# A third w_out tile in the broadcast pool, and residual loads tied to the first square sum, in the FFN down projection of a two-layer decoder trunk

## The chip, the cores and the metric

The kernel runs on one core of a Trainium2 chip. The time is the device time of one execution in microseconds (us); before and after are compared by the median of their runs. Engines are named as in the profile: PE (TensorE), PEld (its weight loads), DVE (VectorE), ACT (ScalarE), POOL (GpSimd) and SP, whose queue issues the DMAs of this kernel. L665 is line 665 of the kernel before. In the changed kernel the same lines have numbers 2 to 7 higher: the residual load is L381 before and L383 after, the matmul of the down projection L665 and L671, the load of H L622 and L624, that of w_out L626 and L632.

## What is computed

Two decoder layers over x of 1024 positions by 1024 channels, all in float32. Layer 0 mixes tokens with a chunked gated MLP, layer 1 with RWKV-7; each goes on with a cross attention into 256 memory rows and a SwiGLU feed-forward block (FFN), and each sub-layer is wrapped in two norms. Cut to what the change touches:

```
def rms_norm(x, g):
    xf = x.astype(jnp.float32)
    y = xf * lax.rsqrt(jnp.mean(xf * xf, axis=-1, keepdims=True) + RMS_EPS)
    return (y * g.astype(jnp.float32)).astype(x.dtype)

def swiglu_ffn(x, w_in, w_out):
    gate, up = jnp.split(x @ w_in, 2, axis=-1)
    return (jax.nn.silu(gate) * up) @ w_out

# every sub-layer:  x <- x + post_norm(f(pre_norm(x)))
```

The hidden width D_FF is 2816, so `w_out` is 2816 by 1024. The down projection is the last product, and the closing of a tile is the post norm, the addition to x (the residual) and the pre norm of the next sub-layer.

## The kernel before

**Numbers.** A float32 matmul is made of three: each operand is split into a rounded high part and a low part (`split`: a cast on ACT, L118, then a subtraction on DVE, L119), and high by high, high by low and low by high are summed in PSUM. In the down projection the high part is called `wh` and the low part `wl`, for H and for the weights alike; each step's two operands are split as a *unit* of two casts and two subtractions.

**The FFN.** `ffn` computes the gate and the up projection column block by column block and writes the hidden values, already combined, to seven DRAM buffers `hd` (`scr<-a` in the profile, L506 to L522). `ffn_out` then forms the down projection as seven products instead of eight (Strassen's scheme over 2 by 2 blocks): products 1, 2, 5, 6, 3, 7, 4 in this order, each in NS = 6 steps over D_FF (step 0 has one block of 128 rows per half, steps 1 to 5 two). A step has 12 or 24 matmuls of 128x128 by 512, so a product has 132. `load(q)` fetches one step's H tile into pool `wr` (3 buffers) and, in products 1, 2, 5 and 6, its rows of w_out. The loads run AHEAD = 3 steps before the matmuls. For product 1 the rows of steps 0 and 1 go into pool `s7` (2 buffers, called `s` in the profile); all other w_out tiles go into the large pool `a` of 32 buffers, which the gate stage also uses. `combine` later forms the other products' weights out of these tiles in place, on DVE. Pool `gb` has two buffers that hold gains broadcast over the partitions; in an FFN one of them holds the gains of its own post norm (`gpost`), the other the gains of the cross attention before it, whose last reader is that sub-layer's end (DVE, L430).

**Closing.** When a product completes a 128 by 512 block of the output, `evac` copies or adds it into tile y, and `finish` squares it on ACT (L677, the sum goes to a column of the group's small tile) and multiplies it by `gpost` on DVE (L678). The output tiles form groups: in layer 0 four groups of two tiles (nn = 2), in layer 1 eight groups of one. When all blocks of a group are there, a task made by `close` is queued: it takes a buffer `xr` per tile from the pool `t4` (4 buffers, called `t` in the profile), loads the residual rows into it from DRAM on SP (L381), forms the norm factor, adds on DVE (L390) and stores on SP (L391). In layer 0 it goes on with the next pre norm (L401, L403) and transposes.

**What sets the order.** The kernel is written as a sequence, with queued tasks run between its pieces (`tick`), but a scheduler decides where an instruction stands on its engine, by what it depends on and by its own estimate of time. An engine, SP included, then takes its instructions in that order. The residual load depends on nothing that the group computes; it needs only a free `t4` buffer, so the scheduler is free to put it far ahead of the rest of `close`. In layer 1 product 4 is split ahead into resident `a` tiles (`resident`), of which most are made while product 7 runs.

## Time and profile before

| | |
|---|---|
| median of 3 runs | 3202.71 us (3199.85 to 3232.83) |
| profiled execution | 3209.07 us, of which the span is 3207.2 us |
| mean granted PE clock in it | 0.967 |
| PE busy | 3080.7 us, 96% of the span |
| DVE, ACT, POOL busy | 1816.4, 1483.7 and 794.9 us |
| down projection, layer 0 | about 1067 us (first L665) to 1310 us |
| down projection, layer 1 | about 2967 us to the end |

Rows of a timeline give the start in us, the time in us, the engine, the line, the operation, what is written from what is read, and how often; in brackets the idle time before the row, and the instruction that ended it. SPq is the queue of SP, a DMA's row there being its issue and not its transfer. The chain that ended last is followed back from the end of the program, and its rows name the piece of work that was then the latest.

### The profile page before, as it was taken

To read this page: it belongs to the slowest core of one execution; us is meant where nothing else is said; L and a number is where in the kernel's file an instruction comes from. 1 tells how busy PE (TensorE), PEld (TensorE's weight loads), DVE (VectorE), ACT (ScalarE), POOL (GpSimd) and SP (SyncE) were. 2 spreads that over 40 slices of the span, in tenths; PEclk is the share of its full clock that TensorE was granted. 3 is DMA by queue.
4 is the path that set the end of the run, shared out by engine and by line. 5 is a ranking of instruction groups with operands and counts; after the bars stand their busy time and mean duration, and the time that the engine had idled before them with its cause. 6 is when DMAs were issued, how large, how long until landed. Compare 5 with 4: busy or idle time off the path is not lost.

```text
span 3207.2 us, 43874 instructions
## 1 busy us (share of the span) xinstructions
PE 3080.7 (96%) x16570; PEld 2519.9 (79%) x16570; DVE 1816.4 (57%) x2594; ACT 1483.7 (46%) x2751; POOL 794.9 (25%) x632
## 2 busy tenths in 40 slices
PE   8999999999999999999989899999999999999998
PEld 6788888778888777878767778887788778888776
DVE  5463544565555476655765667464545755554655
ACT  5433544633333345766753455355545533333443
POOL 0100011345555100111421121123011365554001
PEclk9999999999999999999998889699999999999999
DMA  5622535423333744744857633534553333333633
GB/s 191 204 74 71 192 118 167 158 75 100 105 99 98 251 137 132 226 127 146 266 184 197 191 105 87 150 97 164 180 165 134 110 109 99 99 99 125 233 113 130
DMA packets 434579, 457.59 MB, mean 143 GB/s; under 512 B 77696, under 2 KB 309280, under 8 KB 434368
## 3 DMA queue, kind: packets, MB, share of 16 engines
q1 hardware_dynamic: 427456, 429.62, 42.3%
q0 software_dynamic: 6912, 25.17, 2.5%
q8 instruction: 131, 2.15, 0.3%
q14 instruction: 80, 0.66, 0.1%
HBM read 332.48 MB, written 122.22 MB: 142 GB/s over the span
## 4 chain that ended last, share of the span: by engine, by line
PE 83%; DVE 6%; DMA 5%; issue 2%; ACT 2%; POOL 2%; SPq 1%; DVEq 0%; POOLq 0%; ACTq 0%
PE ps L459 26%; PE ps L148 11%; PE ps L150 11%; PE ps L149 11%; PE ps L665 11%; PE ck L1459 4%; PE ps L1356 2%; DVE wl L119 1%; PE ck L1472 1%; DMA a<-scr 1%; PE ps L1380 1%; DVE a L119 1%; PE ps L274 1%; DMA ld<-scr 1%; ACT wh L118 1%
## 5 line engine op out<-in xcount | busy, mean ns | idle before, releaser
L459 PE MATMUL ps<-a,wh 128*128 128x512 f32 x2464 | 772.3, 398 | 6.6 <-DVE a L119 5.4
L119 DVE TENSOR_TENSOR wl<-wr,wh 128x1024 fp32r<-128x1024 f32 (+1 forms) x417 | 481.5, 1165 | 460.4 <-ACT wh L118 454.9
L118 ACT CAST wh<-wr 128x1024 fp32r<-128x1024 f32 (+1 forms) x417 | 371.0, 901 | 601.1 <-PE ps L665 168.8
L459 PEld LDWEIGHTS ps<-a,wh 128*128 128x128 f32 x2464 | 465.6, 189 | 122.4 <-DVE a L119 7.0
L459 PE MATMUL ps<-a,wl 128*128 128x512 f32 x1232 | 480.7, 398 | 0.9 <-DVE wl L119 0.9
L148 PE MATMUL ps<-a,wh 128*128 128x512 f32 (+1 forms) x848 | 328.5, 392 | 9.7 <-ACT a L118 7.5
L148 PE MATMUL ps<-wh,a 128*128 128x512 f32 x800 | 316.0, 403 | 12.3 <-DVE a L430 4.1
L149 PE MATMUL ps<-a,wh 128*128 128x512 f32 (+1 forms) x848 | 324.9, 384 | 2.4 <-DVE a L119 2.4
L150 PE MATMUL ps<-a,wl 128*128 128x512 f32 (+1 forms) x848 | 324.5, 384 | 2.3 <-DVE wl L119 2.2
L149 PE MATMUL ps<-wl,a 128*128 128x512 f32 x800 | 318.6, 399 | 0.5 <-DVE wl L119 0.5
L150 PE MATMUL ps<-wh,a 128*128 128x512 f32 x800 | 316.1, 399 | 0.2 <-DVE a L119 0.2
L220 POOL TENSOR_TENSOR sm<-sm,mhalf 128x2 f32<-128x2 f32 (+3 forms) x68 | 72.2, 1065 | 922.3 <-DVE sm L240 847.6
L459 PEld LDWEIGHTS ps<-a,wl 128*128 128x128 f32 x1232 | 233.2, 189 | 58.1 <-DVE wl L119 1.4
L119 DVE TENSOR_TENSOR wl<-s,wh 128x512 fp32r<-128x512 f32 (+1 forms) x188 | 202.6, 1091 | 75.0 <-ACT wh L118 71.4
L665 PE MATMUL ps<-wl,wh 128*128 128x512 f32 x588 | 233.6, 397 | 10.3 <-DVE wl L119 10.3
L665 PE MATMUL ps<-wh,wl 128*128 128x512 f32 x588 | 231.9, 394 | 0.0
L118 ACT CAST wh<-s 128x512 fp32r<-128x512 f32 (+1 forms) x188 | 115.8, 633 | 205.2 <-PE ps L459 74.3
L665 PE MATMUL ps<-wh 128*128 128x512 f32 x588 | 198.2, 398 | 11.0 <-ACT wh L118 11.0
L148 PEld LDWEIGHTS ps<-a,wh 128*128 128x128 f32 x848 | 162.0, 192 | 43.5 <-ACT a L118 8.4
L150 PEld LDWEIGHTS ps<-a,wl 128*128 128x128 f32 x848 | 162.1, 191 | 37.0 <-DVE wl L119 4.0
L148 PEld LDWEIGHTS ps<-wh,a 128*128 128x128 f32 x800 | 151.8, 190 | 49.1 <-DVE a L430 5.0
L149 PEld LDWEIGHTS ps<-a,wh 128*128 128x128 f32 x848 | 162.7, 192 | 33.0 <-DVE a L119 2.7
(283 smaller groups left out, 5279.7 us busy)
## 6 DMA issues: line engine op xcount, KB each, us to landing
scr<-a SPq DMA_DIRECT2D x218, 256.0 KB
wr<-in_ffn_w_in SPq DMA_DIRECT2D x92, 512.0 KB
wr<-scr SPq DMA_DIRECT2D x70, 512.0 KB
scr<-t SPq DMA_DIRECT2D x58, 512.0 KB
wr<-in_rw_w_rkv SPq DMA_DIRECT2D x48, 512.0 KB
a<-in_ffn_w_out SPq DMA_DIRECT2D x38, 512.0 KB
ld<-scr SPq DMA_DIRECT2D x72, 256.0 KB
t<-scr SPq DMA_DIRECT2D x34, 512.0 KB
```

Of the source, the lines that this page charges most:

```text
L118: self.nc.scalar.copy(hi, src)
L119: (engine or self.nc.vector).tensor_sub(lo, src, hi)
L148: nc.tensor.matmul(out, lhsT=ah, rhs=bh, start=start, stop=False)
L149: nc.tensor.matmul(out, lhsT=ah, rhs=bl, start=False, stop=False)
L150: nc.tensor.matmul(out, lhsT=al, rhs=bh, start=False, stop=stop)
L220: self.nc.gpsimd.tensor_tensor(out=r, in0=v, in1=self.mhalf[:, 0:n], op=ALU.pow)
L274: nc.tensor.transpose(ps[:, t * P:(t + 1) * P], xs[t][:, k * P:(k + 1) * P], self.ident)
L459: self.nc.tensor.matmul(out, lhsT=a, rhs=b, start=start and k == 0 and (i == 0), stop=k == 3 and i == 2, skip_group_check=True)
L665: nc.tensor.matmul(ps, lhsT=a, rhs=b, start=i in (1, 2, 5) and n == 0 and k == 0 and z == 0, stop=n == NS - 1 and k == steps[n][1] - 1 and ...
L1356: nc.tensor.matmul(ps[:, c * P:(c + 1) * P], lhsT=BK[hs, q * 4 + c, :, :], rhs=AR[hs, q * 4 + c, :, :], start=True, stop=True)
L1380: nc.tensor.matmul(ps[0:64, o:o + 64], lhsT=GA[:, h, q * 4 + c, :], rhs=UV[:, q * 4 + c, h, :], start=True, stop=True)
L1459: mm = lambda o, l, r: nc.tensor.matmul(o, lhsT=l, rhs=r, start=False, stop=True, skip_group_check=True)
```

## The change

Two edits, both in `ffn_out` and in `close`.

1. For product 1 the w_out rows of step 2 go into the second buffer of pool `gb` instead of a buffer of pool `a`. The scheduler can place this load as soon as the cross attention's gains have been read for the last time.
2. `close` gets an argument `begun`: the column that the group's first square sum is written to. Before the residual load of a tile is issued, one element per partition of that column is copied into the first column of its `t4` buffer (DVE, 128x1). The load overwrites the copy, so it has to come after it, and thereby after the first square sum of the group. Other sub-layers call `close` without `begun` and are unchanged in this.

```
-        def close(tiles, hs, s):
+        def close(tiles, hs, s, begun=None):
...
             for t in tiles:
                 xr.append(self.tmp())
+                if begun is not None:
+                    nc.vector.tensor_copy(xr[-1][:, 0:1], begun)
                 nc.sync.dma_start(xr[-1], xin[t * P:(t + 1) * P, :])
...
-                W[b, a, n] = self.s7.tile([P, D], F32, name='s7', tag='s7') if b == a == 0 and n < 2 else self.a32()
+                if b == a == 0 and n < 3:
+                    pool, name = ((self.s7, 's7'), (self.s7, 's7'), (self.gb, 'gb'))[n]
+                    W[b, a, n] = pool.tile([P, D], F32, name=name, tag=name)
+                else:
+                    W[b, a, n] = self.a32()
                 nc.sync.dma_start(view(W[b, a, n], K), wv[b][:, c:c + K, a * 512:a * 512 + 512])
...
-        sums, done = ({}, {})
+        sums, done, begun = ({}, {}, {})
...
                 sums[group] = self.sums(nn)
                 done[group] = 0
+                begun[group] = sums[group][1][:, c:c + 1, tiles.index(t)]
...
-                self.later(close(tiles, [y[x] for x in tiles], s))
+                self.later(close(tiles, [y[x] for x in tiles], s, begun[group]))
```

The scheduler lays the instructions out anew. Four places follow, each before and then after.

SP at the start of layer 0's gate stage (`scr_93` is what the cross attention's closings store, `in_ffn_w_in` the gate stage's weights; layer 1 has the same):

```order
L381 DMA t_5050<-scr_92 128x1024
L471 DMA wr<-in_ffn_w_in 128x8x128 x2
L391 DMA scr_93<-t_4950 128x1024
L391 DMA scr_93<-t_4952 128x1024
L471 DMA wr<-in_ffn_w_in 128x8x128 x2
L391 DMA scr_93<-t_5048 128x1024
L391 DMA scr_93<-t_5050 128x1024
L471 DMA wr<-in_ffn_w_in 128x8x128 x5
```

```order
L383 DMA t_5050<-scr_92 128x1024
L473 DMA wr<-in_ffn_w_in 128x8x128 x2
L393 DMA scr_93<-t_4950 128x1024
L393 DMA scr_93<-t_4952 128x1024
L473 DMA wr<-in_ffn_w_in 128x8x128 x2
L632 DMA gb<-in_ffn_w_out 128x2x512
L393 DMA scr_93<-t_5048 128x1024
L393 DMA scr_93<-t_5050 128x1024
L473 DMA wr<-in_ffn_w_in 128x8x128 x5
```

The load into `gb` is new there, ahead of the last two stores of the cross attention and of the third batch of gate weights.

SP at the start of layer 0's down projection (`wr<-scr_5014` are the H tiles of product 1, `a<-in_ffn_w_out` the w_out tiles; layer 1 has the same):

```order
L626 DMA s_8193<-in_ffn_w_out 128x2x512
L622 DMA wr<-scr_5014 128x2x512 x2
L381 DMA t_9263<-scr_93 128x1024
L506 DMA scr_5014<-a 128x512
L622 DMA wr<-scr_5014 128x2x512
L381 DMA t_9265<-scr_93 128x1024
L381 DMA t_9355<-scr_93 128x1024
L622 DMA wr<-scr_5014 128x2x512 x2
L511 DMA scr_5015<-a 128x512
L512 DMA scr_5017<-a 128x512
L626 DMA a<-in_ffn_w_out 128x2x512
L516 DMA scr_5018<-a 128x512
```

```order
L632 DMA s_8193<-in_ffn_w_out 128x2x512
L624 DMA wr<-scr_5014 128x2x512 x2
L508 DMA scr_5014<-a 128x512
L624 DMA wr<-scr_5014 128x2x512 x3
L513 DMA scr_5015<-a 128x512
L514 DMA scr_5017<-a 128x512
L632 DMA a<-in_ffn_w_out 128x2x512
L518 DMA scr_5018<-a 128x512
```

The residual loads (L381) are gone from here; they now stand among the loads of H for product 5. The first load into an `a` buffer, in the same place behind the stores of `hd`, is that of step 2 before and that of step 3 after.

SP at the end of layer 1 (`out` is the kernel's output, `scr_20997` and `scr_20994`, or 21005 and 21002 after, the H tiles of products 7 and 4):

```order
L391 DMA out<-t_25233 128x1024
L622 DMA wr<-scr_20997 128x2x512
L381 DMA t_25595<-scr_96 128x1024
L391 DMA out<-t_25283 128x1024
L622 DMA wr<-scr_20997 128x2x512
L381 DMA t_25639<-scr_96 128x1024
L391 DMA out<-t_25318 128x1024
L391 DMA out<-t_25362 128x1024
L381 DMA t_25683<-scr_96 128x1024
L381 DMA t_25727<-scr_96 128x1024
L622 DMA wr<-scr_20994 128x512
L622 DMA wr<-scr_20994 128x2x512 x5
```

```order
L393 DMA out<-t_25241 128x1024
L624 DMA wr<-scr_21005 128x2x512
L393 DMA out<-t_25292 128x1024
L624 DMA wr<-scr_21005 128x2x512
L393 DMA out<-t_25328 128x1024
L393 DMA out<-t_25373 128x1024
L624 DMA wr<-scr_21002 128x512
L624 DMA wr<-scr_21002 128x2x512 x5
L383 DMA t_25607<-scr_96 128x1024
L383 DMA t_25652<-scr_96 128x1024
L383 DMA t_25697<-scr_96 128x1024
L383 DMA t_25742<-scr_96 128x1024
```

The four residual loads move from between the stores and the loads of H to behind the last load of H.

DVE in product 7 of layer 0 (`wl<-wr` and `wl<-a` are the two subtractions of a unit; L889, after it L896, scales two tiles of the memory rows for layer 1, which PE then transposes; L390, after it L392, is the closing's addition):

```order
L240 SCALAR_TENSOR_TENSOR sm<-sm 128x2
L403 TENSOR_SCALAR a<-t_9265,sm 128x1024
L119 TENSOR_TENSOR wl<-wr,wh 128x1024
L119 TENSOR_TENSOR wl<-a,wh 128x1024
L240 SCALAR_TENSOR_TENSOR sm<-sm 128x2 x2
L889 SCALAR_TENSOR_TENSOR a<-a,sm 128x1024 x2
L119 TENSOR_TENSOR wl<-wr,wh 128x1024
L390 SCALAR_TENSOR_TENSOR t_9355<-a,sm,t_9355 128x1024
L390 SCALAR_TENSOR_TENSOR t_9357<-a,sm,t_9357 128x1024
L119 TENSOR_TENSOR wl<-a,wh 128x1024
```

```order
L240 SCALAR_TENSOR_TENSOR sm<-sm 128x2
L405 TENSOR_SCALAR a<-t_9266,sm 128x1024
L240 SCALAR_TENSOR_TENSOR sm<-sm 128x2 x2
L896 SCALAR_TENSOR_TENSOR a<-a,sm 128x1024 x2
L119 TENSOR_TENSOR wl<-wr,wh 128x1024
L392 SCALAR_TENSOR_TENSOR t_9357<-a,sm,t_9357 128x1024
L392 SCALAR_TENSOR_TENSOR t_9360<-a,sm,t_9360 128x1024
L119 TENSOR_TENSOR wl<-a,wh 128x1024
```

One unit's two subtractions, which stood right behind L403, now stand behind the scalings and around the two additions. On PE the 16 transposes of the scaled tiles stand one step of product 7 earlier, behind the first four matmuls of the step that uses this unit.

## The prediction

> **What bounds the kernel now.** I read the page's head and its chain first, then who TensorE (PE) waits for, then the places where it waits, engine by engine. The span and the chain's shares by engine:

> ```profile
> span 3207.2 us, 43874 instructions
> ...
> PE 83%; DVE 6%; DMA 5%; issue 2%; ACT 2%; POOL 2%; SPq 1%; DVEq 0%; POOLq 0%; ACTq 0%
> ```

> PE carries 83% of the chain; an edit pays only where PE stands still or runs at a lower clock. The first row of PE's waits, by what ended them (total us, times, longest):

> ```profile
> PE ps L665 <- ACT wh L118: 11.0, 3, 3.9
> ```

> L665 is the matmul of the down projection. Three of its waits end with a cast on ACT and make 11.0 us. Where they lie, in the timeline of PE (start, us, idle before in brackets), followed by windows around them and around one shorter wait (busy us of PE, PEld, DVE, ACT, POOL; granted clock; DMA share; GB/s):

> ```profile
> 1081.87 2.08 PE L665 MATMUL ps<-wh 128*128 128x512 f32 x4 [3.63 <-ACT wh L118]
> ...
> 2981.70 2.08 PE L665 MATMUL ps<-wh 128*128 128x512 f32 x4 [3.87 <-ACT wh L118]
> ...
> 3155.90 2.08 PE L665 MATMUL ps<-wh 128*128 128x512 f32 x4 [3.46 <-ACT wh L118]
> ```

> ```profile
> 1081.87:1090.00 8.13, 8.13 (x25) 6.47 (x26) 3.48 (x3) 2.06 (x3) 0.00 (x0) 0.68 1.06 407
> 2981.70:2988.00 6.30, 6.30 (x21) 5.09 (x22) 3.47 (x3) 1.94 (x2) 0.00 (x0) 0.74 1.05 405
> 3155.90:3161.00 5.10, 5.10 (x16) 4.09 (x17) 3.27 (x5) 2.83 (x4) 0.00 (x0) 0.69 0.61 202
> 1236.25:1242.00 5.75, 5.75 (x18) 4.57 (x19) 3.65 (x5) 4.67 (x12) 0.70 (x1) 0.70 0.59 190
> ```

> The first two waits stand at step 2 (counted from 0) of product 1 in layers 0 and 1, the third in layer 1's product 7. After each PE is busy, but at a clock of 0.68, 0.74 and 0.69, so the wait is paid a second time.

> **Part 1: the third w_out load into the gb buffer.** The chain through the first wait (start, us, what):

> ```profile
> 1073.20 0.69 DVE a L586
> ...
> 1074.76 5.94 DMA a<-in_ffn_w_out
> ...
> 1080.78 1.05 ACT wh L118
> ```

> Step 2's rows go into an "a" buffer that is free only after DVE's last gate product (L586) and the stores behind it; the DMA, the cast and PE follow one after the other. With the rows in gb, loaded at the stage's start, this chain is no longer step 2's. PE ended step 1 at 1081.87 − 3.63 = 1078.24 and could go straight on. Its price: 3.63 idle, and (1 − 0.68) × 8.13 = 2.60 lost at the lower clock: 6.2 us. Layer 1: 3.87 + (1 − 0.74) × 6.30 = 5.5 us.

> What is late next is step 3, whose load is now the first into an "a" buffer. It keeps the old times: issue 1074.76, cast from 1080.78 to 1081.83, and a DVE subtraction behind it. PE's pace comes from a stretch at full clock, 15.40 / 67 = 0.230 us a matmul (first row), the subtraction from the second:

> ```profile
> 3184.76 15.40 PE ps L665 x67
> ```

> ```profile
> 1138.89 1.21 DVE L119 TENSOR_TENSOR wl<-s,wh 128x1024 fp32r<-128x1024 f32 x1
> ```

> Step 2 has 24 matmuls, 5.5 us: step 3 starts at 1078.24 + 5.5 = 1083.8 and has its low half at 1081.83 + 1.21 = 1083.0, its high half before. That is just in time, 0.8 us to spare, so both gains are booked whole; the margin's failure is the first rival. Later steps' loads, a step apart, have one load less ahead.

> The added gb load lies at the gate stage's start on SP:

> ```profile
> 626.18 1.53 SPq L391 DMA_DIRECT2D scr<-t x2
> 628.58 11.05 SPq L471 DMA_DIRECT2D wr<-in_ffn_w_in x3
> ```

> It goes directly ahead of the first of these rows and is 512 KB ahead of what the stage waits for. At the 407 GB/s of the first window above it takes 1.3 us if nothing else moves: between 0 and 1.3 a layer, nearer 0 since the three loads of the second row issue over 11.05 us, waiting for buffers rather than for the DMA. I take +0.3 each, +0.6.

> **Part 2: the residual loads behind a copy.** At the start of the projection they stood in SP's order ahead of wr loads:

> ```profile
> 1057.13 13.77 SPq L381 DMA_DIRECT2D t<-scr x2
> ```

> SP sits 13.77 us here for a t4 buffer. The chain above goes through DVE L586 and not through this row, so I book nothing for its going. It also takes 3 × 512 KB out of the DMA's fullest stretch (share 1.06), which can only help step 3; its value, unknown, lies between 0 and the 0.8 us margin, and I take 0.

> At layer 1's end the same order does cost. SP's timeline, then the chain there, and DVE's release of the slot:

> ```profile
> 3139.97 1.29 SPq L391 DMA_DIRECT2D out<-t x2
> 3146.54 1.55 SPq L381 DMA_DIRECT2D t<-scr x2
> 3148.19 17.68 SPq L622 DMA_DIRECT2D wr<-scr x6
> ```

> ```profile
> 3140.92 6.83 DMA out<-t
> ...
> 3148.19 5.04 DMA wr<-scr
> ```

> ```profile
> 3142.46 1.23 DVE L119 TENSOR_TENSOR wl<-wr,wh 128x1024 fp32r<-128x1024 f32 x1 [1.56 <-ACT wh L118]
> ```

> The residual load waits for the store from its buffer to land (6.83 us), and product 4's first wr load (L622) stands behind it. The wr slot is free at 3142.46 + 1.23 = 3143.69, so without the row ahead the load can go at about 3143.8, 4.4 us earlier. ACT, in order, casts this load ahead of product 7's last two units, and PE waits for those until 3155.90. 4.4 is more than the 3.46 that PE waits, so all of that and (1 − 0.69) × 5.10 = 1.6 go: 5.1. DVE is busy without a break from 3159.72 on, and one wait for it stands there:

> ```profile
> 3164.40 0.50 PE L665 MATMUL ps<-wl,wh 128*128 128x512 f32 x1 [0.41 <-DVE wl L119]
> ```

> When PE comes sooner, such a wait grows; I take off 0.4 for one more: −4.7, between −3.5 (the idle alone) and −5.1. The four loads themselves move behind all wr loads, to about 3167, when the last slots turn over; the stores that use them issue after product 4, 15 us later, so they stay hidden.

> The copies: 16 of 128x1, 8 a layer. The nearest DVE row of such size:

> ```profile
> 1238.99 0.15 DVE L240 SCALAR_TENSOR_TENSOR sm<-sm 128x2 f32<-128x2 f32 x1
> ```

> 16 × 0.15 = 2.4 us of DVE time. On the path lie those at product 2's end, where DVE runs without a break and PE takes wl as it is made:

> ```profile
> 1140.16 0.50 PE L665 MATMUL ps<-wl,wh 128*128 128x512 f32 x1
> ```

> The pair that this matmul needs ended at 1138.89 + 1.21 = 1140.10, 0.06 ahead. Two copies now stand ahead of it, 0.3 us, and slack there is none: between 0.2 and 0.5 a layer, 0.4 taken, +0.8. The others follow gain products at the ends of products 7 and 4, with loads needed later. A copy waits for its buffer's last store; those stores issue a product (30 us) earlier and land in 6.83, so DVE does not stand there.

> **Moved by the scheduler.** In layer 0's product 7 the split of one unit on DVE slides behind two memory scalings (L889) and two closings, and PE's 16 transposes go ahead one step:

> ```profile
> 1246.85 2.48 DVE L889 SCALAR_TENSOR_TENSOR a<-a,sm 128x1024 f32<-128x1024 f32 x2 [0.74 <-POOL sm L220]
> ```

> ```profile
> 1248.00 1.07 PE L665 MATMUL ps<-wh 128*128 128x512 f32 x4
> ...
> 1254.36 1.91 PE L899 MATMUL ps<-ident,a 128*128 128x128 f32 x16
> ```

> Now L889 can start when POOL has answered the two L240, about 1243.6, and end at 1246.0; a split (1.21) to 1247.2, two closings of the kind in the chain (1.2 each) to 1249.6, the second split to 1250.8. PE needs it after the four matmuls from 1248.00 (0.9 us at 0.230) and after the 16 transposes (up to 1.91, the second row; before they stood behind the four of the next step): 1250.6 to 1250.8. So +0.0 to +0.3, with 0.3 taken; were the scalings late, the hole is up to 2.9 and, by the fourth window (clock 0.70 for 5.75 us behind an idle of 2.63), 1.9 more: +4.8 as the upper end.

> ```profile
> 1236.25 0.50 PE L665 MATMUL ps<-wl,wh 128*128 128x512 f32 x1 [2.63 <-DVE wl L119]
> ```

> [...]

> In layer 1's token mixing PE, DVE and ACT have small blocks exchanged (12 of PE's, L1356 and L1363, stand some six matmuls earlier). The stretch:

> ```profile
> 1310.00:2235.00 925.00, 873.52 (x6557) 722.88 (x6557) 563.65 (x1022) 508.64 (x1019) 206.96 (x157) 0.92 0.54 158
> ```

> PE is idle 925 − 873.5 = 51.5 us in it. If a tenth of that comes or goes the price is ±5 us; I take 0. Entering it, a pair of residual loads stands behind a key/value load more: +0.5, between 0 and 1.

> **The sum:** −6.2 − 5.5 − 4.7 + 0.6 + 0.8 + 0.3 + 0.5 = −14.2 us. The profiled execution took 3209.07 us (1.9 beyond its span), so 3194.9, a ratio of 0.9956; on the median of the runs, 3202.71, that is 3188.5, forecast as 3189.

> **Rivals.** (a) Step 3's wait takes the place of step 2's. For: 0.8 us of margin, one "a" load behind the same DVE product, in a full DMA. Against: 1.5 MB less traffic. If it lands 2.5 us late, 1.7 us of idle and about 1.9 of clock come back in each layer: 3189 + 7 = 3196. (b) The front change does not do what it says: the gb buffer, last read by cross attention, is refilled late or the cast sits in ACT's order behind another load, and only the tail gains: −4.7 + 2.2 = −2.5, 3200. Against: SP's order has the load at the stage's start. (c) The other side: the moved block in token mixing has to wait for DVE. The page has such waits for L1537, at most 2.4 us:

> ```profile
> PE ps L1356 <- DVE sm L1537: 3.7, 2, 2.4
> ```

> PE takes its matmuls in order, so all behind it wait too; in the recurrence's 8 head pairs that is at most 8 × 2.4 = 19 us, 3189 + 19 = 3208. It ends slower than before from six such waits on (14.2 / 2.4). Against: the blocks changed places by a few matmuls, and the trace has but two of these waits. (d) The new places fill holes instead: −5 to −10 there, 3181.

> **How the numbers follow.** The forecast has 0.58 (3184 to 3194), (a) 0.14, (b) 0.08, (c) 0.10, (d) 0.10. The range reaches from (d)'s 3178 to 3206, short of (c)'s end: about 0.85. What a measurement can tell from no change is about 1%, 32 us: faster means below 3170.7, slower above 3234.7. No case reaches either with its own price; I leave 0.03 for (d) doubled, 0.02 for (c) with a further stall, 0.95 within.

> **What would show it.** Right: no PE idle over 1 us at step 2 in either layer, the gb load landed long before; step 3's four matmuls start at once; a clock of 1.0 behind; at the tail a wr load right behind the stores, no residual load between, and PE unbroken through product 7 into 4. Wrong: an idle before step 3 (a), an idle at product 2's end or in product 7 of layer 0 over 0.5 us, a DVE copy with a long wait before it, or a token-mixing stretch more than 5 us off 925 us. The forecast falls if that stretch changes by more than the three waits gave.

## The result and the profile after

| | before | after |
|---|---|---|
| median of 22 runs each | 3212.06 us (3193.51 to 3234.38) | 3191.89 us (3179.28 to 3211.27) |
| ratio, with its 95% interval | | 0.9939 (0.9921 to 0.9957) |
| span of the profiled execution | 3207.2 us | 3188.9 us |

0.61% less is 19.6 us on the median, with an interval of 14 to 25 us. The sum forecast 14.2 us, which is just inside the interval, and 3191.89 lies 3 us above the forecast's 3189. That it lies so near is in part luck: the median of before is 9.4 us higher with 22 runs than with the 3 that the forecast started from, and the gain is 5 us larger than forecast. The head of the page of after, and the first rows of PE's waits in it (what waited, for whom; total us, times, longest):

```profile
span 3188.9 us, 43900 instructions
...
PE 3076.4 (96%) x16570; PEld 2519.2 (79%) x16570; DVE 1826.3 (57%) x2610; ACT 1484.8 (47%) x2751; POOL 796.7 (25%) x632
```

```profile
PE ps L671 <- DVE wl L119: 11.3, 8, 2.7
PE ps L254 <- DVE a L359: 9.7, 2, 8.1
PE ps L148 <- ACT a L118: 8.5, 5, 5.2
```

Before, a row of 11.0 us in three waits stood at the top: the down projection's matmul waiting for a cast on ACT. It is gone. Of the 26 instructions more, 16 are the copies (DVE's count goes from 2594 to 2610). At step 2 and step 3 of layer 0's product 1, PE's timeline of after shows the first four matmuls of each step, with no idle time in brackets; below it are the splits on ACT and on DVE, the DMA issues on SP, and two windows (busy us of PE, PEld, DVE, ACT, POOL; granted clock; DMA share; GB/s):

```profile
1076.51 1.07 PE L671 MATMUL ps<-wh 128*128 128x512 f32 x4
...
1081.95 1.07 PE L671 MATMUL ps<-wh 128*128 128x512 f32 x4
```

```profile
1071.02 1.05 ACT L118 CAST wh<-gb 128x1024 fp32r<-128x1024 f32 x1 [0.75 <-PE ps L461]
1076.48 1.05 ACT L118 CAST wh<-wr 128x1024 fp32r<-128x1024 f32 x1 [4.41 <-PE ps L671]
1079.05 1.05 ACT L118 CAST wh<-a 128x1024 fp32r<-128x1024 f32 x1 [1.51 <-DMA a<-in_ffn_w_out]
```

```profile
1077.57 2.21 DVE L119 TENSOR_TENSOR wl<-wr,wh 128x1024 fp32r<-128x1024 f32 x1 [4.12 <-ACT wh L118]
1080.13 1.23 DVE L119 TENSOR_TENSOR wl<-a,wh 128x1024 fp32r<-128x1024 f32 x1 [0.35 <-ACT wh L118]
```

```profile
1055.14 16.97 SPq L624 DMA_DIRECT2D wr<-scr x3
...
1073.23 0.48 SPq L632 DMA_DIRECT2D a<-in_ffn_w_out x1
```

```profile
1074.00:1090.00 16.00, 16.00 (x72) 13.25 (x71) 7.35 (x6) 6.10 (x6) 4.47 (x4) 1.00 0.96 357
2970.00:2986.00 16.00, 16.00 (x72) 13.27 (x71) 8.15 (x6) 6.10 (x6) 3.35 (x3) 1.00 0.92 333
```

The gb tile is cast at 1071.02, long before step 2 needs it. The first load into an "a" buffer, now step 3's, is issued at 1073.23 and cast at 1079.05; its low part is ready at 1080.13 + 1.23 = 1081.36, and step 3 starts at 1081.95. PE is busy for all 16 us of both windows at a clock of 1.00; before, the clock in the 8 us behind the wait was 0.68. SP still stands for 16.97 us at 1055, now at H loads where it stood at residual loads, and PE does not wait; the copies alone, below, show that step 2 did not wait for this block before either.

The tail, in SP's timeline of after:

```profile
3127.91 1.55 SPq L393 DMA_DIRECT2D out<-t x2
3131.93 15.13 SPq L624 DMA_DIRECT2D wr<-scr x6
3154.83 5.18 SPq L383 DMA_DIRECT2D t<-scr x4
```

The H loads of product 4 follow the stores 2.5 us behind (3131.93 − 3129.46), where before they came 6.9 us behind (3148.19 − 3141.26), after the residual loads. PE has its wait of 2.7 us at the start of product 7, as before, and none from there on.

**Where the time went.** All these kernels run 16570 matmuls on PE. Compared place by place, by shape and tile names, the order of PE is that of before at all but 485 places in after, 1292 in the gb tile alone and 1234 in the copies alone; the gb load late has the order of after at every place. The start of the matmul with the same number, compared between a run and the first profile of before, tells in which stage a difference arises. The table is worked out so from the traces, in us; minus is less time than in the first profile of before. The columns are stages of that profile: (a) 0 to 633, (b) 633 to 1062, layer 0's gate stage, (c) 1062 to 1137, its products 1 and 2, (d) 1137 to 1694, (e) 1694 to 2211, the RWKV recurrence, (f) 2211 to 2531, (g) 2531 to 2959, layer 1's gate stage, (h) 2959 to 3033, its product 1, (i) 3033 to 3127, (j) the rest, the tail.

```
                     a     b     c     d     e     f     g     h     i     j    all
before again       -1.5  +0.2  +0.5  +0.5  +6.5  -3.2  +0.7  +1.4  +0.0  -3.2   +1.8
after              -3.2  +1.6  -6.4  +0.8  +0.4  -1.0  +1.3  -5.7  +0.2  -6.5  -18.3
after again        -0.5  +0.6  -6.4  +0.0 +16.4  -3.7  +1.4  -5.7  +0.1  -6.4   -4.3
gb tile alone      -2.2  +0.6  -6.4  -0.3 +22.6  -2.5  +3.2  -5.7  +0.0  -4.4   +4.9
copies alone       -0.6  +1.5  -0.8  -1.4 +25.1  -0.9  +3.1  -0.0  +0.2  -6.5  +19.7
copies alone again +0.2  +0.2  +0.1  -0.4  +1.0  +0.0  +1.6  +0.6  +0.1  -6.5   -3.1
gb load late       -3.1  -0.0  -6.4  -0.3  +7.2  -0.6  -0.2  -5.7  +0.1  -6.6  -15.7
```

Three columns, c, h and j, carry the change: -6.4, -5.7 and -6.5. Column e, where nothing of the change is computed, is larger than all of them together in some runs. The scheduler has moved blocks there, though: 399 of the 485 places lie in it in after, 1144 in the gb tile alone and 974 in the copies alone. The experiments below take that apart.

### The profile page after: what moved, and what is told of

Its sections match the earlier page's. It is cut to its first block, busy times and chain, and to the rows that moved or that the text cites. A ratio compares the mean times of both kernels' runs of the same rounds, so it can differ in the third digit from the quotient of the medians.

```text
span 3188.9 us, 43900 instructions
## 1 busy us (share of the span) xinstructions
PE 3076.4 (96%) x16570; PEld 2519.2 (79%) x16570; DVE 1826.3 (57%) x2610; ACT 1484.8 (47%) x2751; POOL 796.7 (25%) x632
## 5 line engine op out<-in xcount | busy, mean ns | idle before, releaser
L119 DVE TENSOR_TENSOR wl<-wr,wh 128x1024 fp32r<-128x1024 f32 (+1 forms) x417 | 486.1, 1176 | 458.9 <-ACT wh L118 454.5
L118 ACT CAST wh<-wr 128x1024 fp32r<-128x1024 f32 (+1 forms) x417 | 371.1, 901 | 601.4 <-PE ps L671 168.1
L148 PE MATMUL ps<-wh,a 128*128 128x512 f32 x800 | 314.9, 402 | 13.4 <-ACT t L1201 4.0
L220 POOL TENSOR_TENSOR sm<-sm,mhalf 128x2 f32<-128x2 f32 (+3 forms) x68 | 70.8, 1045 | 902.8 <-DVE sm L240 827.0
L119 DVE TENSOR_TENSOR wl<-s,wh 128x512 fp32r<-128x512 f32 (+1 forms) x188 | 201.6, 1087 | 73.9 <-ACT wh L118 70.8
L118 ACT CAST wh<-s 128x512 fp32r<-128x512 f32 (+1 forms) x188 | 115.5, 633 | 207.9 <-PE ps L461 75.2
```

The costliest lines, as they stand in the source:

```text
L118: self.nc.scalar.copy(hi, src)
L119: (engine or self.nc.vector).tensor_sub(lo, src, hi)
L148: nc.tensor.matmul(out, lhsT=ah, rhs=bh, start=start, stop=False)
L220: self.nc.gpsimd.tensor_tensor(out=r, in0=v, in1=self.mhalf[:, 0:n], op=ALU.pow)
```

## The experiments

**The kernel before, once more.** No edit.

> The kernel before, unchanged, profiled once more. In the trace of after, PE stood 3.2 us earlier by 190 us of the span and 1.5 us earlier between 2404 and 2463 us, in places whose order the change leaves alone. Theory (those two belong to the execution and not to the change): this run differs from the first profile of before by some us in the same places, above all before PE's first L788, where that profile idles 5.9 us, and by less than 0.5 us over each of the two down projections. Rival (they come from the change): this run agrees with the first profile there within 0.5 us.

Its waits at the three places, in PE's timeline:

```profile
1080.87 2.07 PE L665 MATMUL ps<-wh 128*128 128x512 f32 x4 [3.91 <-ACT wh L118]
...
2985.51 2.07 PE L665 MATMUL ps<-wh 128*128 128x512 f32 x4 [4.07 <-ACT wh L118]
...
3157.96 1.21 PE L665 MATMUL ps<-wh 128*128 128x512 f32 x4 [0.50 <-ACT wh L118]
```

The theory held for the places outside the change: columns a and f differ by 1.5 and 3.2 us in one and the same program, and PE's first L788 idles 3.74 us here instead of 5.89. It did not hold for "less than 0.5" in the down projections: product 1 of layer 1 took 1.4 more, and the third wait is 0.50 instead of 3.46. The chains of the two profiles of before tell why: the store that the residual load waited for took 6.83 us in the first profile and the H load behind it 5.04 (both rows stand in the prediction), and less here.

```profile
3145.93 5.02 DMA out<-t
...
3151.40 3.90 DMA wr<-scr
```

That is 1.81 and 1.14 us less, together 2.95 of the 2.96 us by which the wait is shorter.

**The gb tile alone.** The close is called without `begun`:

```
-                self.later(close(tiles, [y[x] for x in tiles], s, begun[group]))
+                self.later(close(tiles, [y[x] for x in tiles], s))
```

> The third w_out tile in the gb buffer alone; the residual loads stand as in the kernel before. Theory (the two edits act apart): the idle times of 3.63 and 3.87 us at step 2 of product 1 are gone, PE gains about 6 us in layer 0 and 5.6 us in layer 1 there, it loses 1.6 and 1.3 us at the start of the two gate stages, and the 3.46 us wait in layer 1's product 7 stays: some 9 us in all less than before. Rival (the gb tile works only with the residual loads out of the way): with 1.5 MB more in the DMA's fullest stretch step 3's rows come late, a wait of 1 to 3 us appears before step 3, and the gain in each down projection's start is 2 to 4 us instead of 6.

Median 3210.35 us of 10 runs, ratio to before 0.9996 (0.9967 to 1.0025). The two waits at step 2 are gone and no wait stands before step 3, with the residual loads still in the way; the window over that stretch:

```profile
1074.00:1090.00 16.00, 16.00 (x72) 13.28 (x71) 7.41 (x6) 6.10 (x6) 4.41 (x4) 1.00 1.03 380
```

PE is as unbroken as in after, though the DMA's share is 1.03 instead of 0.96. So the rival fell: 1.5 MB more in the DMA there does not make step 3 late. The theory was wrong about the tail: the wait in layer 1's product 7 was to stay, and it is gone (column j, -4.4). The scheduler has put one H load between the last two residual loads here, though nothing was edited for it:

```profile
3154.08 0.33 SPq L383 DMA_DIRECT2D t<-scr x1
3154.51 0.38 SPq L624 DMA_DIRECT2D wr<-scr x1
3155.32 0.32 SPq L383 DMA_DIRECT2D t<-scr x1
```

The time as a whole contradicted the theory too: 9 us less were expected, none were measured. In the trace the gains are there (columns c, h and j), and 22.6 us more in column e stand against them.

**The copies alone.** Step 2's tile goes to the pool `a` again:

```
-                if b == a == 0 and n < 3:
+                if b == a == 0 and n < 2:
```

> The residual loads behind the copy alone; step 2's rows in an a buffer as before. Theory: the 3.46 us wait in layer 1's product 7 is gone and PE gains 6.5 us over that tail, no loss at the gate stages' start, and the waits at step 2 of product 1 stay within 0.5 us of 3.63 and 3.87, since neither SP's 13.77 us nor the DMA's load of 1.5 MB was what step 2 waited for: 5 to 7 us less than before. Rival (the residual loads delayed step 2): these two waits get shorter by 1 us or more each, and the whole gain is 9 us or more.

```profile
1082.98 2.07 PE L671 MATMUL ps<-wh 128*128 128x512 f32 x4 [3.80 <-ACT wh L118]
...
3007.57 1.78 PE L671 MATMUL ps<-wh 128*128 128x512 f32 x4 [3.72 <-ACT wh L118]
```

The waits at step 2 stay, within 0.2 us of 3.63 and 3.87, and the tail gains 6.5: the theory held at these places, and SP's long block and the residual loads had no part in step 2's wait. It did not hold at the starts of the gate stages (columns b and g, +1.5 and +3.1 where no loss was expected), nor for the time: median 3217.46 us of 10 runs, ratio 1.0041 (1.0009 to 1.0073), slower where 5 to 7 us less were expected. Column e has 25.1 us more.

**The gb load held back.** One element per partition is copied from step 0's tile, so the load waits for that one:

```
                     W[b, a, n] = pool.tile([P, D], F32, name=name, tag=name)
+                    if n == 2:
+                        nc.vector.tensor_copy(W[b, a, n][:, 0:1], W[0, 0, 0][:, 0:1])
```

> The changed kernel, but the load into the gb buffer has to wait: one element per partition of step 0's tile is copied into its first column before, so it is issued with product 1's first loads instead of at the gate stage's start. Theory (the 1.6 and 1.3 us that PE loses in the first 60 us of the gate stages come from 512 KB ahead of the gate weights): that loss is gone in both layers, POOL's first L488 sum starts 1.1 us earlier against PE than in the changed kernel, and the starts of the down projections keep their gain of about 6 us: 2.5 to 3 us less than the changed kernel. Rival 1 (the loss is one execution's): the gate stages start as in the changed kernel. Rival 2 (the late load lands late): a wait at step 2 of more than 1 us takes the gain back.

Median 3188.51 us of 10 runs, ratio 0.9934 (0.9908 to 0.9960): not to be told from the changed kernel's 0.9939. Columns b and g are -0.0 and -0.2, as the theory says, and c and h keep the gain, so the load is early enough there. But the copies alone, which have no gb load at all, lost 1.5 and 3.1 us in the same columns. What differs in b and g is not tied to the load by these runs.

**The same kernels again, for the recurrence.** No edits against the two kernels named.

> The kernel with the copies alone, unchanged, profiled once more. Its recurrence stretch (1694 to 2211 us in the kernel before, 516.6 us) took 541.8 us the first time. Theory (the length there follows the granted clock, which differs from execution to execution of one program by 10 us and more): the stretch lies anywhere from 517 to 545 us, at least 5 us off 541.8, and the difference is in the granted clock, with PE busy throughout. Rival (the moved instructions make it): within 3 us of 541.8 again.

> The changed kernel, unchanged, profiled once more. The recurrence stretch took 517.0 us the first time. Theory (execution to execution): it differs by 3 us or more, in the granted clock. Rival (the new order is a good one there): within 3 us of 517.0. Both: the local terms repeat within 0.5 us but for the tail, where the kernel before itself had 3.46 and then 0.5 us of wait.

The recurrence in six profiles, by windows from the same matmul to the same matmul: before, before again, copies alone, copies alone again, after, after again.

```profile
1694.07:2210.69 516.62, 489.66 (x4801) 412.01 (x4800) 305.79 (x756) 242.49 (x634) 111.22 (x109) 0.88 0.48 131
```

```profile
1693.71:2216.81 523.10, 497.07 (x4802) 418.40 (x4800) 305.33 (x758) 243.12 (x634) 109.61 (x109) 0.86 0.47 129
```

```profile
1692.75:2234.53 541.78, 518.70 (x4802) 434.89 (x4800) 307.74 (x758) 243.97 (x635) 111.56 (x109) 0.83 0.46 126
```

```profile
1694.08:2211.69 517.61, 495.87 (x4802) 415.60 (x4800) 307.44 (x758) 243.93 (x635) 111.27 (x109) 0.87 0.48 132
```

```profile
1686.97:2204.02 517.05, 494.08 (x4802) 415.75 (x4800) 308.17 (x756) 243.44 (x634) 110.35 (x109) 0.87 0.47 131
```

```profile
1687.74:2220.79 533.05, 509.80 (x4802) 429.81 (x4800) 307.29 (x758) 243.81 (x634) 110.02 (x108) 0.84 0.46 127
```

The same program takes 541.8 us and then 517.6, another 517.0 and then 533.0. The number of matmuls is the same and the work of DVE and ACT nearly so; PE's busy time moves with the granted clock, 0.83 against 0.87. Idle time is 22 to 27 us in all six. Both theories held against their rivals as these were put: the length of this stretch changes by 16 and 24 us between two executions of one program, through the clock, so one profile each can hide or feign more than the whole gain.

This does not show that the order has no part. The gb tile alone and the gb load late were timed in ten runs each against the same runs of before, and their intervals, 0.9967 to 1.0025 and 0.9908 to 0.9960, do not overlap. Their medians are 21.8 us apart, and without column e their profiles differ by 5 us only. The two kernels with the same order on PE, after and the gb load late, are both some 20 us faster than before; the two whose order in column e differs at more than twice as many places are not faster. So the recurrence seems to be longer on average in some orders than in others, beside its swing from execution to execution. No run gave one kernel the order of another, so the cause is not shown.

**RWKV left out.** Without the recurrence that spread should go. The kernel before and the changed one, with this edit:

```
-            T.rwkv(W, T.rwkv_params(cols[:, 16:]), lambda: mem_kv(1), mk(3))
+            T.gmlp(I['gm_w_in'][0], I['gm_b_in'][0], I['gm_ln_b'][0], I['gm_w_s'][0], I['gm_b_s'][0], I['gm_w_out'][0], cols[:, 0:8], cols[:, 8:16], lambda: mem_kv(1), mk(3))
...
-            T.fp32_in = n == 2
+            T.fp32_in = False
```

> The kernel before with layer 1's token mixing (RWKV-7) left out and a second gated MLP with layer 0's weights in its place, so the output is another function. It is the partner of the next run: between the two, PE's order differs in the down projections alone. Both theories expect the waits of the kernel before: about 3.6 to 4.1 us at step 2 of product 1 in each layer, and 0.5 to 3.5 us in layer 1's product 7.

> The changed kernel with the same replacement of layer 1's token mixing. Theory (the local terms, as the traces so far sized them, are the change's own effect): -6.4 and -5.7 at the starts of the two down projections, -3.3 to -6.5 at the tail, +1.6 and +1.3 at the gate stages' starts, within 0.5 elsewhere: 12.5 to 16 us less than its partner in the trace and in the median. Rival (a part of the 20 us by which the changed kernel was faster lies in these stages and was overlooked): 18 us or more between the two.

Then the kernel before in this form once more, and each part in it:

> The kernel before with the second gated MLP in RWKV's place, once more, as the partner of the next three on the same chip. Expected: a median within 4 us of the 2575.0 of the first time, waits of 3.4 to 4.1 us at step 2 of product 1 in both layers, and a tail of layer 1 that varies with how long the last store of a residual buffer takes to land.

> The gb tile alone, with the second gated MLP in RWKV's place; the residual loads stand as before. Theory (the parts add up; the full kernel's time hid this under the recurrence's spread): 9 to 12 us less than its partner, -6.4 and -5.7 in the trace at the two starts. Rival (the part alone gains nothing, as its time in the full kernel said): within 4 us of its partner.

> The copies alone, with the second gated MLP in RWKV's place. Theory: only layer 1's tail gains, -1 to -6.5 us by how long the store takes in the partner's execution, and the copies cost 0.3: 1 to 5 us less than its partner; no wait in product 7 behind the residual loads. Rival (the part alone costs, as its time in the full kernel, 0.4% above, said): 4 us or more above its partner.

> Both edits with the gb load held back to product 1's first loads, with the second gated MLP in RWKV's place. Theory (512 KB ahead of the gate weights cost PE 1 us or more a layer): 1.5 to 3 us less than the changed kernel's 12.6 us gain left, so 14 to 16 us less than its partner, and POOL's first sum starts about 10.7 us after PE's first gate matmul instead of 11.9. Rival (what differs at the gate stage's start is one execution's): 11 to 14 us less than its partner, with POOL's first sum as early.

| RWKV left out | median, us | runs | against its partner |
|---|---|---|---|
| before | 2575.00 | 4 (2572.37 to 2580.20) | |
| both edits | 2562.39 | 5 (2558.61 to 2564.83) | -12.6 |
| before, again | 2575.78 | 5 (2565.94 to 2578.84) | |
| gb tile alone | 2562.09 | 4 (2560.37 to 2566.42) | -13.7 |
| copies alone | 2574.47 | 4 (2570.97 to 2576.18) | -1.3 |
| both, gb load late | 2561.58 | 4 (2558.19 to 2562.94) | -14.2 |

The partner of the last three rows is before, again. The three kernels with the gb tile lie apart from the three without it but for one pair of runs: the slowest of the one kind, 2566.42, is above the fastest of the other, 2565.94. By the medians the gb tile is worth 12 to 14 us here; the copies' 1.3 is within the spread of their runs. The traces agree. Worked out as in the table above, against the first profile of before in this form, the starts of the two down projections give -7.1 to -7.2 and -5.7 to -5.8 us in the three kernels with the gb tile, and between -1.2 and +0.8 in the others. Both edits gain 13.9 us in the trace and 12.6 in the median, within the 12.5 to 16 expected. The rival of that run, 18 us or more in these stages, fell, and the parts add up within about 2.5 us (-13.7 and -1.3 against -12.6 and -14.2), so the rivals of the gb tile alone and the copies alone fell as well. The gb tile alone gained a little more than the 9 to 12 expected. In the first profile of before in this form the third wait does not occur at all (0.31 us is the longest in the tail after product 7's start), and the copies' gain is small for that: SP has one H load of product 4 between the last stores and the last two residual loads here,

```profile
2510.37 1.38 SPq L391 DMA_DIRECT2D out<-t x2
2513.91 0.33 SPq L622 DMA_DIRECT2D wr<-scr x1
2514.98 1.56 SPq L381 DMA_DIRECT2D t<-scr x2
```

where the full kernel has the residual loads ahead of all six. So these runs bound the tail's worth in the full kernel from below only. The gb load late, -14.2, lies just inside its theory's 14 to 16 and just outside the rival's 11 to 14, and its own runs are 4.8 us apart, so it decides nothing: its POOL starts the gate stage's sums 10.4 and 11.7 us behind PE's first gate matmul, its partner without any gb load 11.7 and 11.7.

## Why the prediction was right, step by step

- **Step 2's wait, -6.2 and -5.5:** measured -6.4 and -5.7 (columns c and h), in each of the four profiles of the full kernel with the gb tile. The waits and the lower clock behind them both went, as the term said. In each of the seven profiles without the gb tile, four of the full kernel and three of the form without RWKV, the waits are there, at 3.4 to 4.1 us.
- **Step 3 just in time:** the margin was given as 0.8 us; it is 1081.95 − 1081.36 = 0.6 to the step's first matmul. The first rival did not come, not even with the residual loads left in.
- **SP's block of 13.77 us booked at nothing:** right; the copies alone leave step 2's waits as they were.
- **The tail, -4.7:** the mechanism was right, the size off. Against the execution that it was read from the change gave -6.5: the 0.4 taken off for a DVE wait was a loss that did not come, and that execution's own waits of 0.41 and 0.31 us went as well. Of the 0.7 that is left, 0.45 lies ahead of the wait, where before again gains the same without an edit. Against the second execution of before it gave 6.5 − 3.2 = 3.3. The term hangs on how long a store and the H load behind it take to land (6.83 and 5.04, 5.02 and 3.90 us in two profiles), and one execution was taken as if it were all. The gb tile alone already has -4.4 there, by the order on SP that the scheduler gave it; over that the copies bring 2.1 in these profiles.
- **The copies at product 2's end, +0.8:** the mechanism was right, the size three times too large. Column c ends just ahead of this place. Right behind it, at 1139 to 1141 us of before and at 3038 to 3040 in layer 1, PE loses 0.11 to 0.13 us in each of the five profiles with the copies, and 0.01 at most in before again and the gb tile alone: about 0.25 for both layers. DVE's rows of after show that two copies push the next row back by 0.12 us, not by the 0.3 booked:

```profile
1128.01 0.20 DVE L382 COPY t<-sm 128x1 f32<-128x1 f32 x2
1128.13 0.68 DVE L697 TENSOR_TENSOR a<-ps,a 128x512 f32<-128x512 f32 x1
```

- **The gb load at the gate stage's start, +0.6:** left open. Columns b and g are +0.6 to +3.2 in the three profiles with the early load, and +0.2 to +3.1 in those with copies alone or before again; POOL's first sum starts 11.8 to 12.0 us behind PE's first gate matmul with the load and 10.5 to 11.7 without it, or with it late, in the full kernel, but 10.4 to 14.0 without it or with it late in the form without RWKV. A price of about 1 us a layer may be in there; the runs don't separate it from what changes by itself.
- **Product 7 of layer 0, +0.3:** +0.2 net, but not as it was told. In the first profile of after a wait of 1.49 us does stand behind the moved split, one of the signs that were to show the prediction wrong, though with no drop of the clock behind it; and the wait of 2.63 us ahead of it, which cost PE a clock of 0.79 in 11 of the 14 profiles, cost none in this one:

```profile
1228.43 0.50 PE L671 MATMUL ps<-wl,wh 128*128 128x512 f32 x1 [2.63 <-DVE wl L119]
...
1242.86 0.50 PE L671 MATMUL ps<-wl,wh 128*128 128x512 f32 x1 [1.49 <-DVE wl L119]
```

```profile
1228.43:1236.43 8.00, 8.00 (x35) 6.63 (x36) 4.64 (x8) 7.16 (x16) 2.07 (x3) 1.00 0.38 129
```

  In the second profile of after the first wait is again 2.63 us, the clock behind it is lower, and the second wait is absent:

```profile
1230.10:1238.10 8.00, 8.00 (x28) 6.42 (x29) 4.64 (x8) 7.12 (x16) 2.07 (x3) 0.79 0.38 141
```

  28 matmuls in 8 us against 35: PE arrives later and finds the split ready. DVE sets the end of this stretch either way, which is why a step can show a new wait and cost nothing.
- **Token mixing, 0 with ±5:** the bound was too narrow. In the recurrence the same program differs by 16 and by 24 us between two executions, by the clock and not by waits for moved blocks, so rival (c) named a place that matters and a cause that is not the one shown. The sign given for it, a stretch more than 5 us off, could not tell: from 1310 to 2235 us the first profile of after is 1.6 us longer than before, its second 12.8, and before again 5.5. Rival (b) fell: the load into gb came in time.

**The whole.** In the full kernel the terms that were seen twice come to -6.4 − 5.7 − 3.3 to -6.5, with at most 1 us a layer against them: -13.4 to -18.6. The measured 14 to 25 us fits this; without RWKV it was 12.6, with a smaller tail. That the change's median lies at 19.6, and that each part alone showed no gain or a loss in the full kernel, is not settled. In the traces each part's gains are there, and the time is lost in the recurrence. The intervals of the timed runs make chance alone unlikely; a recurrence that is longer on average in the order of the kernels with one part alone would explain it, and that order does differ most there, but no run tried the order by itself.

## What to carry to other kernels

PE's waits of 3.63 and 3.87 us, each ended by a cast behind a transfer, were worth 6.4 and 5.7 us here, the wait and the slow clock behind it; give the late operand a buffer that was free before, and then compute what is late next, to the half microsecond, from the rows of the first. A load that needs only a free buffer can be hoisted by a scheduler to where it blocks the queue for the loads behind it (SP stood 13.77 us at two of them here); a cheap write that it must follow holds it back (two copies pushed DVE's next row back by 0.12 us). Before a gain of half a per cent is looked for in the whole time, compare two profiles of one and the same program stage by stage: where a stage differs by more than the gain, take that stage out of both kernels and measure the rest. An edit in one stage can also move instructions in another, as the scheduler did here, so compare the orders there too before a difference is put down to the edit.

## What the runs showed of the hardware

**The clock behind one and the same wait differs.** In all 14 profiles PE had the same wait at the start of product 7 in each layer, 2.63 and 2.71 us. In the 8 us behind it the clock was 0.62 to 0.82 in 23 of these 28 places and 1.00 in 5; in layer 0 the changed kernel had 1.00 in its first profile and 0.79 in its second. Behind waits of 1.04 to 1.09 us (four in each profile's down projections) it was 1.00 every time, behind the down projections' waits of 3.4 to 4.1 us never above 0.81. What decides between the two outcomes behind 2.63 and 2.71 us was not shown.

**A low clock can hold with PE busy.** In the recurrence of the gb tile alone a window of 65.6 us shows PE busy throughout at 0.65:

```profile
1909.86:1975.48 65.62, 65.62 (x616) 57.58 (x607) 26.77 (x71) 24.24 (x59) 7.50 (x8) 0.65 0.36 101
1918.40:1959.30 40.90, 40.90 (x321) 36.17 (x320) 17.22 (x40) 12.56 (x23) 5.35 (x6) 0.50 0.36 101
```

```profile
2039.50:2066.80 27.30, 27.30 (x184) 23.86 (x184) 9.18 (x24) 5.93 (x12) 1.11 (x2) 0.50 0.41 116
```

```profile
1930.06:1953.94 23.88, 23.88 (x169) 21.41 (x170) 11.50 (x27) 7.63 (x14) 3.20 (x4) 0.50 0.44 120
```

The matmuls of the last row write 128x128 elements at most, most of them 64x128, 128x64 or 32x32, where those of the down projection write 128x512. What holds the clock down was not tried.

**A split twice as long.** The first of the two DVE rows quoted for after takes 2.21 us, where such a subtraction takes 1.22 elsewhere. POOL works just then:

```profile
1077.41 1.29 POOL L523 TENSOR_TENSOR a<-a 128x512 f32<-128x512 f32 x1
```

It ends at 1078.70, and from there to DVE's end at 1079.78 it is 1.08 us, nearly a whole subtraction. The same pair of rows stands in layer 1 of this profile, and it has 339 subtractions of this size. Seven of them took 1.68 to 2.30 us; each ran beside a POOL operation of 128x512 that had begun before it, and ended 1.08 us behind that one's end. The 300 with no POOL arithmetic beside them took 1.21 to 1.23, the other 32 took 1.21 to 1.24. Why these seven are held up was not tried.
